# A gated linear-attention stage: where in program order the next head's set-up stands, and how many buffers its tiles have

## The chip, the cores and the metric

The kernel runs on one core of one Trainium2 chip. The core's engines work in parallel, each through its own list of instructions in a fixed order: PE (TensorE) multiplies matrices, DVE (VectorE) and ACT (ScalarE) work element by element, POOL (GpSimd) does further element-wise work, and SP only issues DMA transfers between the chip's memory (HBM) and the on-chip buffers. An instruction that has to wait holds back everything behind it on its engine. The metric is device time in microseconds (us) for one execution.

## The reference

Two blocks of two layers each run one after the other on 512 tokens of width 1024, in float32. The stage that is changed is in the second block. Each of its two layers is a SwiGLU feed-forward, then a mixer, then another SwiGLU. The mixer joins a neighbourhood attention (8 heads of width 64) and a gated linear attention (GLA, 4 heads, keys of width 64, values of width 128), and `w_out` projects both back to width 1024:

```
def step(state, inp):                      # one chunk of 64 tokens, per head
    qi, ki, vi, gi = inp
    b = cumsum(gi)                         # log decays
    inter = (qi * exp(b)) @ state
    decay = exp(where(mask, b[:, None] - b[None], -inf))
    a = einsum('td,sd,tsd->ts', qi, ki, decay)
    state = exp(b_last)[:, None] * state + (ki * exp(b_last - b)).T @ vi
    return state, inter + a @ vi
o = rmsnorm(gla(q, k, v, gf, forward) + gla(q, k, v, gb, backward)) * silu(r)
x = x + concat([neighbourhood_attention, o]) @ w_out
```

## The kernel before

Activations stay in on-chip memory as four tiles of 128 tokens. Every large product is done as three matmuls on a high and a low part of each operand (`mm3`, lines 150 to 152). The parts are made by a cast on ACT (`whi`, line 111) and a subtraction on DVE (`wlo`, line 112). Weights come by DMA into `raw` buffers (two of them, line 125) and are split from there.

The mixer stage is `mix`. It first projects the values (`gla_v`), the gates (`gates`, which leaves the summed log decays `b` of the four heads in tiles `gb`), `gla_q` and `gla_k` (one DRAM buffer, `gla_qk`) and the output gate (`gla_r`, with a Silu on ACT); v, q, k and r are written to DRAM and read back per head. Then `interleave` draws from two generators in turn, 36 steps of `heads()` against 24 of `others()`.

`heads()` runs `gla_head` for each of the four GLA heads. The forward direction is kept in partitions 0 to 63 and the backward direction in 64 to 127. One head has three parts, and 9 steps:

- **Set-up** (1 step, lines 1321 to 1363): four DMAs for q and k (`gq`, `gk`, each loaded twice, for the two directions) and one for v (`gv`); the shifted decays `gR` (two DVE copies and a POOL memset); `geq`, an exponential of `b` on ACT; the decays to the end of each 128-token block (`gd`, two DVE subtractions, lines 1337 and 1338), their exponential on ACT (line 1340) and its product with k on DVE (line 1341); four PE transposes, an ACT copy, four PE matmuls with v (line 1349); the states `gst` (six DVE instructions, lines 1353 to 1360, reading PSUM); and `gzi`, q times `geq` (line 1362).
- **Seven levels** (7 steps, lines 1366 to 1388): for block sizes 64, 32, ... 1 the scores between the two halves of each block. A level is a DVE subtraction (line 1370), two ACT exponentials into `ge` (1373, 1374), a POOL memset and two POOL products with k into `gzk` (1376 to 1378), a DVE product of `ge` with q in place (1379; it follows the POOL products, which read the same tile), PE matmuls (1383), and a masked DVE copy into `gA` (1387).
- **End** (1 step, lines 1389 to 1408): state and score matmuls (1391, 1392), the norm, the gate, transposes, and the split into a pair of `gkt` tiles for `w_out`.

`gq`, `gk`, `gR` and `geq` have one buffer each; `gd`, `gv`, `gzk`, `gzi` and `gst` have two, `ge` four. `others()` projects the neighbourhood attention's values (`tokens_out`, line 1161) and its q and k (`na_qk`, line 1181), loads what that attention needs (`na_setup`, 14 DMAs at line 1193), and then runs its first four heads (`na_heads`: scores 1238, transposes 1260, outputs 1267) beside the projection of GLA heads 0 and 1 through `w_out`.

The instructions are not issued in exactly the order in which the program writes them. A planner orders each engine's list when the kernel is built: an instruction written earlier has the higher priority, but the planner, going by its own estimates of durations, lets a later one go ahead when its operands and its tile's buffer are free first. A tile whose tag has one buffer can only be written when the last reader of the tile before it is through. On the chip the list is then fixed.

Of the kernel before, what the change touches and what calls it, by code (L numbers as in the profile page):

```python
# [10 lines left out]
F32 = mybir.dt.float32  # L11
# [6 lines left out]
S = 512  # L18
# [1051 lines left out]
GH = 4  # L1070
# [10 lines left out]
class Block2(Block1):  # L1081
# [5 lines left out]
    def gates(self, pool, l, w_in, hT):  # L1087

        nc = self.nc
        d = self.d  # L1090
        v = w_in[:, 3072:3104].rearrange("(k p) n -> p k n", p=P)
        raw = self.wpool.tile([P, 2048], F32, name=self.n("raw"), tag="raw", bufs=2)
        rv = raw[:, :1024].rearrange("p (k n) -> p k n", k=KD)
        with nc.allow_non_contiguous_dma(reason="32 columns"):
            for i in range(4):
                nc.sync.dma_start(rv[:, :, i * 32 : i * 32 + 32], v)
        w = self.wsplit([raw[:, :1024]])[0]
        gw = pool.tile([32, GH, 2, 64], F32, name=self.n("gw"), tag="gA")
        nc.gpsimd.memset(gw, 0.0)
        gb = pool.tile([P, GH], F32, name=self.n("gb"), tag="gbias")  # L1100
        with nc.allow_non_contiguous_dma(reason="gate weights"):
            for i, n in enumerate("fb"):
                nc.sync.dma_start(gw[i * 16 : i * 16 + 16, :, i, :], d[f"w_gate_{n}_2"][l].rearrange("r (h e) -> r h e", h=GH))
                nc.sync.dma_start(gb[i * 64 : i * 64 + 64, :], d[f"b_gate_{n}_2"][l].rearrange("(h e) -> e h", h=GH))
        scan = pool.tile([P, S], F32, name=self.n("scan"), tag="gst", bufs=2)
        nc.sync.dma_start(scan, d["c_scan"])
        ps = self.proj_T(w, hT)
        code = pool.tile([32, S], F32, name=self.n("code"), tag="gR")
        nc.scalar.copy(code, ps[:32])
        es, bs = [], []  # L1110
        for h in range(GH):
            z = self.ps(tag="BD")
            nc.tensor.matmul(z, gw[:, h].rearrange("r a e -> r (a e)"), code, start=True, stop=True)
            a = pool.tile([P, S], F32, name=self.n("gt"), tag="ge", bufs=4)
            nc.scalar.activation(a, z, AF.Abs, bias=gb[:, h : h + 1])
            m = pool.tile([P, S], F32, name=self.n("gb"), tag="gb", bufs=4)
            nc.vector.tensor_scalar(m, z, gb[:, h : h + 1], 0.0, ALU.add, ALU.min)
            es.append(a)
            bs.append(m)
        for a in es:  # L1120
            nc.scalar.activation(a, a, AF.Exp, scale=-1.0)
        for a in es:
            nc.scalar.activation(a, a, AF.Ln, bias=1.0)
        for a, m in zip(es, bs):
            nc.vector.tensor_sub(a, m, a)
            nc.vector.tensor_tensor_scan(m[:64], scan[:64], a[:64], 0.0, ALU.mult, ALU.add)
            nc.vector.tensor_tensor_scan(m[64:, ::-1], scan[64:, ::-1], a[64:, ::-1], 0.0, ALU.mult, ALU.add)
        return bs
# [189 lines left out]
    def gla_head(self, pool, h, b, qk, vs, rs, mask, sgn, kts, new_k):  # L1318
        nc = self.nc
        new = lambda tag, bufs: pool.tile([P, S], F32, name=self.n(tag), tag=tag, bufs=bufs)  # L1320
        q, k = new("gq", 1), new("gk", 1)
        for t, m in ((q, 0), (k, 256)):
            for i in range(2):
                nc.sync.dma_start(t[i * 64 : i * 64 + 64, :], qk[m + h * 64 : m + h * 64 + 64, :])
        v3 = pool.tile([P, NT, P], F32, name=self.n("gv"), tag="gv", bufs=2)
        nc.sync.dma_start(v3, vs[:, h * P : (h + 1) * P].rearrange("(t p) e -> p t e", p=P))
        R = new("gR", 1)
        nc.vector.tensor_copy(R[:64], b[:64])
        nc.vector.tensor_copy(R[64:, 0:511], b[64:, 1:512])
        nc.gpsimd.memset(R[64:, 511:512], 0.0)  # L1330

        eq = new("geq", 1)
        nc.scalar.activation(eq, b, AF.Exp, scale=1.0 / 16)
        D = new("gd", 2)
        bt = b.rearrange("p (t s) -> p t s", t=NT)
# [68 lines left out]
        k = new_k()  # L1404
# [4 lines left out]
    def mix(self, l, xs, norm, nxt):  # L1409
# [4 lines left out]
        with self.scope("mix") as pool:  # L1414
            new_k = lambda: Split(*(pool.tile([P, 512], F32R, name=self.n("gkt"), tag="gkt", bufs=10) for _ in range(2)))
            mask = pool.tile([P, len(LEVELS), P], I32, name=self.n("gmask"), tag="gmask")
            nc.sync.dma_start(mask, d["c_gmask"].rearrange("l p t -> p l t"))
            both = pool.tile([P, 8], F32, name=self.n("both"), tag="both")
            sgn, ngain = both[:, 0:2], both[:, 4:8]
            for i in range(2):  # L1420
                for c in range(2):
                    nc.gpsimd.memset(sgn[i * 64 : i * 64 + 64, c : c + 1], (1.0 if i == c else -1.0) / 16)
            gain = pool.tile([P, P], F32, name=self.n("ggain"), tag="ggain")
            nc.sync.dma_start(gain, d["gla_gain_2"][l].unsqueeze(0).to_broadcast([P, P]))
            with nc.allow_non_contiguous_dma(reason="512 gains"):
                nc.sync.dma_start(ngain, d["na_gain_2"][l].rearrange("(k p) -> p k", p=P))
            hT = norm.hT
            vs, rs, nv = (self.dr(n, [S, 512]) for n in ("gla_v", "gla_r", "na_v"))
            nqk = self.dr("na_qk", [8, P, S])
            for _ in self.tokens_out(pool, w_in, 2048, hT, vs, None, norm.finish):  # L1430
                pass
            bs = self.gates(pool, l, w_in, hT)
            qk = self.gla_qk(pool, w_in, hT)
            for _ in self.tokens_out(pool, w_in, 2560, hT, rs, gain):
                pass
            kts = []
            st = {}

            def gout(a, tag):
                ws = self.wrows(w_out, [512 + (a + i) * P for i in range(2)])  # L1440
                return self.down_steps(xs, [self.cols(k) for k in kts[a : a + 2]], ws, tag=tag)

            def heads():
                for h in range(GH):
                    yield from self.gla_head(pool, h, bs[h], qk, vs, rs, mask, sgn, kts, new_k)

            def others():
                yield from self.tokens_out(pool, w_in, 1024, hT, nv)
                yield from self.na_qk(pool, w_in, hT, nqk)
                st["na"] = self.na_setup(pool, l, nqk, nv)  # L1450
                g = gout(0, "A")
                for _ in range(4):
                    next(g)
                for _ in self.na_heads(pool, st["na"], (0, 1), new_k, "A", "C", "C"):
                    next(g, None)
                    yield
                for _ in g:
                    pass

            interleave(heads(), 36, others(), 24)  # L1460
            na = st["na"]
            interleave(self.na_heads(pool, na, (2, 3), new_k, "AB", "C", "D"), 8, gout(2, "AB"), 8)
            ws = self.wrows(w_out, [k * P for k in range(4)], scales=[ngain[:, k : k + 1] for k in range(4)])
            self.down(xs, [self.cols(k) for k in na["K"]], ws, self.na_scale(pool, na), nxt.after)
# [108 lines left out]
```

## Time and profile before

| | |
|---|---|
| time, median of 3 runs | 3266.24 us (3262.35 to 3266.77) |
| the profiled execution's own time | 3260.75 us |
| its span, first to last instruction | 3259.0 us |
| PE busy | 3194.2 us (98%) |
| DVE busy | 2168.5 us (67%) |
| ACT busy | 1391.3 us (43%) |
| POOL busy | 481.0 us (15%) |
| mean granted TensorE clock | 0.991 of full speed |

The two interleaved stretches lie at about 1660 to 1840 us and 2656 to 2840 us of the span. A busy PE is one with a matmul in flight; at a granted clock below 1.00 the same matmuls take longer and are still counted as busy, so idle time and clock have to be read side by side.

### The profile page before, as it was taken

The page shows a single profiled execution, that of the slowest core. Times are in us where ns is not written, and L with a number is a line of the kernel's source. Part 1 is how long each engine was busy: PE and PEld are TensorE (multiplying, and loading weights), DVE is VectorE, ACT ScalarE, POOL GpSimd, SP SyncE. Part 2 cuts the span into 40 slices and gives each one's busy share as a digit, 9 for nine tenths or more (in the row PEclk, how much of TensorE's full clock was granted, in tenths as well). Part 3 has the DMA queues.
Part 4 walks back from the last instruction along what each step waited for, and adds up shares of the span by engine and source line. Part 5 has one row for each costly group of instructions (what it writes and reads, how often), then busy time and mean ns, then how long its engine had stood idle before and what let it go on. Part 6 is the DMA issues. An engine that isn't in the chain of part 4 may idle for free. (4 is left out here: it accounts for less than half of the span.)

```text
span 3259.0 us, 39483 instructions
## 1 busy us (share of the span) xinstructions
PE 3194.2 (98%) x15381; PEld 2645.9 (81%) x15381; DVE 2168.5 (67%) x3054; ACT 1391.3 (43%) x2130; POOL 481.0 (15%) x554
## 2 busy tenths in 40 slices
PE   8999999999999999999999999999999999999999
PEld 8777888887788888888878788888888887788887
DVE  5566677767867776666576656665666657656665
ACT  5465444446744444333354533333333354443332
POOL 0022222111222210000134300000000025400000
PEclk9999999999999999999999999999999999999999
DMA  6311333222233323232444232324223253332231
GB/s 214 93 40 38 111 104 104 82 81 90 77 131 104 104 78 123 78 104 90 129 133 148 69 110 91 117 78 135 92 78 108 85 164 122 111 104 91 78 109 60
DMA packets 265882, 330.51 MB, mean 101 GB/s; under 512 B 20872, under 2 KB 198240, under 8 KB 265696
## 3 DMA queue, kind: packets, MB, share of 16 engines
q1 hardware_dynamic: 265696, 328.00, 31.2%
q8 instruction: 121, 1.98, 0.2%
q14 instruction: 65, 0.53, 0.1%
HBM read 313.28 MB, written 14.68 MB: 101 GB/s over the span
## 5 line engine op out<-in xcount | busy, mean ns | idle before, releaser
L111 ACT CAST whi<-raw 128x1024 fp32r<-128x1024 f32 x398 | 414.0, 1050 | 428.0 <-PE psC L152 128.7
L112 DVE TENSOR_TENSOR wlo<-raw,whi 128x1024 fp32r<-128x1024 f32 x402 | 499.1, 1247 | 116.4 <-ACT whi L111 108.6
L150 PE MATMUL psA<-hThi,wlo 128*128 128x512 f32 (+1 forms) x1264 | 473.2, 375 | 2.7 <-ACT hThi L111 1.8
L151 PE MATMUL psA<-hTlo,whi 128*128 128x512 f32 (+1 forms) x1264 | 472.1, 374 | 0.8 <-DVE hTlo L112 0.7
L150 PE MATMUL psC<-hThi,wlo 128*128 128x512 f32 (+1 forms) x1264 | 471.2, 373 | 0.5 <-ACT hThi L111 0.5
L152 PE MATMUL psA<-hThi,whi 128*128 128x512 f32 (+1 forms) x1264 | 471.2, 373 | 0.0
L151 PE MATMUL psC<-hTlo,whi 128*128 128x512 f32 (+1 forms) x1264 | 470.5, 372 | 0.0
L152 PE MATMUL psC<-hThi,whi 128*128 128x512 f32 (+1 forms) x1264 | 470.1, 372 | 0.0
L111 ACT CAST whi<-b 128x1024 fp32r<-128x1024 f32 (+1 forms) x238 | 237.6, 998 | 283.7 <-PE psA L152 91.7
L112 DVE TENSOR_TENSOR wlo<-b,whi 128x1024 fp32r<-128x1024 f32 (+1 forms) x238 | 275.8, 1159 | 68.5 <-ACT whi L111 66.8
L172 POOL TENSOR_TENSOR rv<-msv,mhalf 128x1 f32<-128x1 f32 (+1 forms) x60 | 45.7, 762 | 1737.8 <-DVE msv L169 1737.8
L150 PEld LDWEIGHTS psA<-hThi,wlo 128*128 128x128 f32 x1264 | 239.3, 189 | 45.8 <-ACT hThi L111 4.8
L151 PEld LDWEIGHTS psA<-hTlo,whi 128*128 128x128 f32 x1264 | 239.2, 189 | 43.9 <-DVE hTlo L112 2.5
L152 PEld LDWEIGHTS psA<-hThi,whi 128*128 128x128 f32 x1264 | 239.1, 189 | 41.3
L151 PEld LDWEIGHTS psC<-hTlo,whi 128*128 128x128 f32 x1264 | 238.4, 189 | 42.0 <-issue 0.8
L150 PEld LDWEIGHTS psC<-hThi,wlo 128*128 128x128 f32 x1264 | 238.4, 189 | 41.9 <-ACT hThi L111 1.0
L152 PEld LDWEIGHTS psC<-hThi,whi 128*128 128x128 f32 x1264 | 238.3, 189 | 41.3
L359 DVE SCALAR_TENSOR_TENSOR x<-psB,x 128x512 f32<-128x512 f32 x272 | 181.0, 686 | 136.2 <-PE psB L152 135.2
L150 PE MATMUL psB<-whi,kb 128*128 128x512 f32 x608 | 238.0, 391 | 0.0
L151 PE MATMUL psB<-wlo,kb 128*128 128x512 f32 x608 | 236.7, 389 | 0.0
L152 PE MATMUL psB<-whi,kb 128*128 128x512 f32 x608 | 236.6, 389 | 0.0
L359 DVE SCALAR_TENSOR_TENSOR x<-psD,x 128x512 f32<-128x512 f32 x204 | 135.9, 686 | 112.4 <-PE psD L152 112.4
(506 smaller groups left out, 5783.8 us busy)
## 6 DMA issues: line engine op xcount, KB each, us to landing
raw<-in_ffn_wg_dram SPq DMA_DIRECT2D x44, 1024.0 KB
raw<-in_ffn_wu_dram SPq DMA_DIRECT2D x44, 1024.0 KB
b<-in_ffn_wd_dram SPq DMA_DIRECT2D x72, 512.0 KB
raw<-in_w_up_dram SPq DMA_DIRECT2D x32, 1024.0 KB
b<-in_w_down_dram SPq DMA_DIRECT2D x56, 512.0 KB
raw<-in_w_in_dram SPq DMA_DIRECT2D x40, 512.0 KB
raw<-in_w_out_dram SPq DMA_DIRECT2D x32, 512.0 KB
raw<-in_lru_w_in_dram SPq DMA_DIRECT2D x10, 1024.0 KB
```

The costliest lines, as they stand in the source:

```text
L111: self.nc.scalar.copy(out.hi, src)
L112: self.nc.vector.tensor_sub(out.lo, src, out.hi.bitcast(F32))
L150: nc.tensor.matmul(out, lhsT.lo, rhs.hi, start=start, stop=False, skip_group_check=more)
L151: nc.tensor.matmul(out, lhsT.hi, rhs.lo, start=False, stop=False, skip_group_check=more)
L152: nc.tensor.matmul(out, lhsT.hi, rhs.hi, start=False, stop=stop, skip_group_check=more)
L172: nc.gpsimd.tensor_tensor(r, ms, e, ALU.pow)
L359: nc.vector.scalar_tensor_tensor(x, p, scale, x, ALU.mult, ALU.add)
```

## The change

The generators of all four heads are made at once. Head 0's set-up comes first; then each head's steps are drawn as before, but after the level with index 2 the set-up of the next head is drawn. The number of steps stays 36. `gq`, `gk`, `gR` and `geq` get two buffers (8 KB more per partition in all); `code` in `gates` shares the tag `gR` and is given the same count.

```diff
@@ gates
-        code = pool.tile([32, S], F32, name=self.n("code"), tag="gR")
+        code = pool.tile([32, S], F32, name=self.n("code"), tag="gR", bufs=2)
@@ gla_head
-        q, k = new("gq", 1), new("gk", 1)
+        q, k = new("gq", 2), new("gk", 2)
...
-        R = new("gR", 1)
+        R = new("gR", 2)
...
-        eq = new("geq", 1)
+        eq = new("geq", 2)
@@ mix, heads()
+                gens = [self.gla_head(pool, h, bs[h], qk, vs, rs, mask, sgn, kts, new_k) for h in range(GH)]
+                next(gens[0])
+                yield
                 for h in range(GH):
-                    yield from self.gla_head(pool, h, bs[h], qk, vs, rs, mask, sgn, kts, new_k)
+                    for i, _ in enumerate(gens[h]):
+                        yield
+                        if i == 2 and h + 1 < GH:
+                            next(gens[h + 1])
+                            yield
```

## Rows read from the trace of the kernel before

**Rows 1.** The page's busy times by engine: us, share of the span, instructions.

```profile
PE 3194.2 (98%) x15381; PEld 2645.9 (81%) x15381; DVE 2168.5 (67%) x3054; ACT 1391.3 (43%) x2130; POOL 481.0 (15%) x554
```

**Rows 2.** Engine timeline of PE: start, us, instruction, [idle before it and its releaser].

```profile
1701.84 2.05 PE L1383 MATMUL psB<-ge,gzk 128*128 128x128 f32 x8 [3.52 <-DVE ge L1379]
...
1703.54 0.77 PE L150 MATMUL psC<-whi,hTlo 128*128 128x512 f32 x1
...
2700.60 2.00 PE L1383 MATMUL psB<-ge,gzk 128*128 128x128 f32 x8 [3.51 <-DVE ge L1379]
```

**Rows 3.** 4-us stretches: length; PE, PEld, DVE, ACT, POOL busy (count); PEclk; DMA share; GB/s.

```profile
1700.00:1704.00 4.00, 2.17 (x9) 2.20 (x10) 4.00 (x5) 0.83 (x3) 1.14 (x1) 0.57 0.25 66
...
1704.00:1708.00 4.00, 4.00 (x12) 3.11 (x12) 4.00 (x6) 0.88 (x2) 2.32 (x3) 0.58 0.49 135
...
2700.00:2704.00 4.00, 3.40 (x12) 3.14 (x13) 4.00 (x6) 0.91 (x2) 1.19 (x2) 0.58 0.22 66
```

**Rows 4.** Timeline of DVE, first of the two layers.

```profile
1680.59 1.23 DVE L112 TENSOR_TENSOR wlo<-raw,whi 128x1024 fp32r<-128x1024 f32 x1 [6.50 <-ACT whi L111]
...
1695.43 0.68 DVE L1337 TENSOR_TENSOR gd<-gb 64x512 f32<-64x512 f32 x1
...
1696.12 1.25 DVE L1338 TENSOR_TENSOR gd<-gb 64x512 f32<-64x512 f32 x1
...
1697.40 1.22 DVE L1370 TENSOR_TENSOR gd<-gb,gR 128x512 f32<-128x512 f32 x1
...
1699.16 1.28 DVE L1370 TENSOR_TENSOR gd<-gb,gR 128x512 f32<-128x512 f32 x1
...
1700.37 1.32 DVE L1379 TENSOR_TENSOR ge<-ge,gq 128x512 f32<-128x512 f32 x1
...
1707.56 0.68 DVE L1341 TENSOR_TENSOR ge<-ge,gk 128x512 f32<-128x512 f32 x1
...
1723.64 0.35 DVE L1360 SCALAR_TENSOR_TENSOR gst<-gst,geq,psD 64x128 f32<-64x128 f32 x1
```

**Rows 5.** Timeline of ACT around the same gap.

```profile
1697.48 0.63 ACT L1340 ACTIVATE ge<-gd 128x512 f32<-128x512 f32 x1 [5.73 <-PE psA L152]
...
1698.02 1.98 ACT L111 CAST whi<-raw 128x1024 fp32r<-128x1024 f32 x2
```

**Rows 6.** Timeline of POOL around the same gap.

```profile
1696.87 1.20 POOL L1378 TENSOR_TENSOR gzk<-gk,ge 64x256 f32<-64x256 f32 x1
```

**Rows 7.** Timeline of PE where the neighbourhood attention begins, both layers.

```profile
1794.16 1.13 PE L1238 MATMUL psA<-hTlo,hThi 64*128 64x256 f32 x4 [2.13 <-DMA hThi<-na_qk]
...
2794.46 2.07 PE L1238 MATMUL psA<-hTlo,hThi 64*128 64x256 f32 x4 [4.20 <-DMA hThi<-na_qk]
```

**Rows 8.** 4-us stretches behind these two waits.

```profile
1796.00:1800.00 4.00, 4.00 (x11) 2.38 (x10) 3.80 (x10) 1.09 (x4) 3.69 (x4) 0.52 0.73 259
...
1800.00:1804.00 4.00, 4.00 (x18) 3.24 (x17) 2.20 (x6) 1.57 (x5) 2.37 (x3) 0.63 0.02 4
...
2792.00:2796.00 4.00, 1.54 (x4) 1.17 (x4) 0.00 (x0) 0.00 (x0) 0.00 (x0) 0.60 0.83 220
...
2796.00:2800.00 4.00, 4.00 (x11) 2.45 (x10) 2.75 (x7) 1.09 (x4) 3.16 (x4) 0.54 0.69 238
```

**Rows 9.** Timeline of SP (DMA issues): one early stretch, and before that wait.

```profile
1668.24 6.87 SPq L125 DMA_DIRECT2D raw<-in_w_in_dram  x4
...
1781.60 6.22 SPq L1193 DMA_DIRECT2D hThi<-na_v  x10
...
1787.87 0.45 SPq L1225 DMA_DIRECT2D hThi<-na_qk  x1
...
1788.41 1.12 SPq L1324 DMA_DIRECT2D gq<-gla_qk  x2
```

**Rows 10.** Timeline of PE: two levels of the last head in the neighbourhood attention.

```profile
1814.97 1.95 PE L1383 MATMUL psB<-ge,gzk 128*128 128x128 f32 x16
```

**Rows 11.** A 4-us stretch in the neighbourhood attention of the second layer.

```profile
2844.00:2848.00 4.00, 4.00 (x17) 3.58 (x18) 1.88 (x10) 1.28 (x3) 0.00 (x0) 0.50 0.00 0
```

## The prediction

> **What bounds the kernel now.** I read the page's busy times first, then the waits of PE, then stretches of 4 us with the granted clock, and last the timelines of the other engines around each PE gap. PE is busy for 98% of the span [rows 1], and the sum of the matmuls does not change here. So only two things can be won or lost: time in which PE stands idle, and time in which it runs at the lower of its two clock levels (1.2 instead of 2.4 GHz), which follows a gap. In the two mixer stages these sit at few places, and two of them touch what is moved.
>
> Place A is inside the levels of head 0, in both layers. PE idles 3.52 and 3.51 us before a level's score matmuls, released by the DVE product of line 1379 [rows 2]. The granted clock falls at once: 0.57 and 0.58 over two stretches of 4 us in the first layer, 0.58 over one in the second [rows 3]. A stretch at clock c loses (1 - c) x 4 us of full-speed work: 1.72 + 1.68 + 1.68 = 5.1 us. With the idle time A holds 3.52 + 3.51 + 5.1 = 12.1 us.
>
> Place B is where the neighbourhood attention begins: PE waits 2.13 and 4.20 us for its q tile from DRAM [rows 7], and then runs at 0.52 and 0.63 in the first layer, 0.60 and 0.54 in the second [rows 8]: 1.92 + 1.48 + 1.60 + 1.84 = 6.8 us of lost clock. The 0.60 row holds part of the wait itself, so that is a little high; B holds about 2.13 + 4.20 + 6.8 = 13.1 us.
>
> **What makes place A.** The planner already draws head 1's set-up forward, but only when head 0 has released its single `gR` and `ge` and `gd` buffers. The two subtractions of lines 1337 and 1338 then run at 1695.43 and 1696.12, in the middle of head 0's last levels, and head 1's first level subtractions follow at 1697.40 and 1699.16 [rows 4]. The product of line 1379 for head 0's next level has its POOL operand at 1696.87 + 1.20 = 1698.07 [rows 6], yet starts at 1700.37, since it is queued behind these. ACT is held too: its list has the exponential of line 1340 next, which starts at 1697.48, right after line 1338 ends at 1697.37, after 5.73 us of idling; the row names an old PE release, but what came last is the subtraction. Two weight casts are queued behind it [rows 5], and PE's next weights come from these, at 1703.54 [rows 2]. So one late set-up holds both of the things that PE could do next.
>
> **The change, part by part.**
>
> *Set-up earlier, in two buffers (place A).* Head 1's set-up is now written after head 0's third level, and with a second `gR` it need not wait for head 0's last level subtraction. What leaves the crowded stretch: two subtractions, 0.68 + 1.25 = 1.93 us as they ran there, and two copies into `gR`, of the same 64 partitions x 512 and so about 0.68 each by the row of line 1337, 1.4 together: 3.3 us of DVE. What may enter, because the products and states of head 1 now come before head 0's levels 3 to 6 as well: two products of 0.68 and six state instructions of at most 0.35 each [rows 4], 1.4 + 2.1 = 3.5 us. On DVE's sum that is a draw. The gain depends on some of it going into the 6.50 us in which DVE idled at 1674 to 1680 [rows 4], and on ACT's exponential being ready when its turn comes. The best case: line 1379 starts at 1698.07, ends 0.68 later at 1698.75 (the row of line 1341, the same shape); PE ran dry at 1701.84 - 3.52 = 1698.32. So 0.4 us of gap stays per layer, and if so short a gap leaves the clock alone, 12.1 - 0.8 = 11.3 us are won. The worst case within this step is 0: another set-up instruction stands in the same place. I take 8, nearer to the upper end, because the hold of ACT's list goes away with the early subtraction, whatever DVE's sum does.
>
> *The same for the last head (place B).* q and k of head 3 are issued at 1788.41, behind ten of `na_setup`'s DMAs and the attention's q [rows 9], because the single `gq` was still read by head 2. With two buffers and the new place in the program, head 3's loads come before `na_setup`: by the draw of 36 steps against 24 the set-up of head 3 is step 23, and `others()` reaches `na_setup` and the first attention unit at its step 17, when 25 steps of `heads()` have been drawn. (Before, the set-up was step 28.) The DMA wait itself does not shrink, since the attention's q was issued ahead of `gq` already. What changes is that PE has something to do in it: a level is 0.98 us of matmuls by the row of two levels in 1.95 [rows 10], and two to five ready levels fill 2.13 and 4.20 us. Fully filled, B gives up to 13.1; not filled at all, 0. Whether the planner places the levels ahead of the waiting matmul depends on its own estimate of that DMA, so I take half, 6.5.
>
> *What it costs.* Work that fills B is taken from the attention units behind it, where head 3's levels stand between the units now. I put 2 us against that; the bound is in the rival below. The set-up's DMAs are four issues of about 0.56 (1.12 for two [rows 9]) and one for v: 2.2 to 2.8 us on SP, now in front of some weight loads. SP spends 6.87 us on four weight issues at 1668.24 [rows 9], far more than four issues take, so it waits there for `raw` buffers and a further issue in that wait costs nothing; if that cover is gone, the next weights come up to 2.8 us later, once per layer, 5.6 in all. I take 0. The second `geq`, `gR` for `code` and 8 KB more per partition cost no instruction; where tiles of the following stage now lie over those of the mixer, a wait could arise that no row shows. I take 0 for it, with the 0.3 to 0.4 us of a short PE gap as one end and one gap of A's size, 3.5 us plus clock, as the other.
>
> **A rule weighed against the rows.** Line 1337 took 0.68 us and line 1338, of the same shape, 1.25. Line 1370 took 1.22 at 1697.40 while POOL's product of line 1378 ran from 1696.87 to 1698.07 [rows 4, 6]: the DVE instruction ended 0.55 us after POOL's did, as if it had stood still until then. The Trainium skill, page "SBUF — State Buffer", section "Who interferes with whom", says that DVE with two on-chip inputs and a reading GpSimd instruction share a port pair, that whoever starts first keeps it for its whole instruction, and that the other fully blocks. The trace agrees by that row. By that rule moving DVE work among POOL's products can cost more than its own duration, which speaks against this change; as a mechanism of this kernel it is a rival below.
>
> The sum: -8 - 6.5 + 2 = -12.5 us. Against the profiled execution's own 3260.75 us that is 3248.3. That execution is 5.5 us under the median of the runs, so against the median the forecast is 3266.24 - 12.5 = 3253.7, say 3254.
>
> **Rivals.**
>
> *All of it.* A and B are both emptied, nothing is given back: -11.3 - 13.1 = -24, and with 2 to 4 us of small new gaps about -20: 3246. For it: all rows of A and B name resources that are doubled or loaded earlier. Against it: the planner fixes each list by its own estimates, and new lists have new gaps.
>
> *It does not do what it says.* The planner had already drawn the set-up forward, and the DVE draw of 3.3 against 3.5 leaves A as it was; B's matmul keeps its place in PE's list. About -2: 3264.
>
> *The lock eats it.* Six instructions per set-up with two on-chip inputs or a copy (two copies, two subtractions, two products) each lose 1.25 - 0.68 = 0.57 us beside POOL's products: 3.4 us for a head, where DVE is late once per layer, 6.8 in all. Of -12.5 about -5 is left: 3261. For it: the rows above. Against it: four of the six already run beside POOL.
>
> *Slower: the attention loses its filler.* After B the attention units form a chain (scores, softmax, transposes, outputs), and PE is kept busy in it by head 3's seven levels, 7 x 0.98 = 6.9 us, and the projection. If the levels have all run by the time the projection's first part is through, the later units wait for their own chain: at most 6.9 us of idling per layer, and a gap there can drop the clock, as one did in the second layer (0.50 over a stretch of 4 us [rows 11], 2 us lost in that row alone, and two or three such rows). With 6.9 + 4 = 11 per layer and only A won, -8 + 22 = +14; with half of that idling and of the clock +3. I take +8: 3274. It decides from the point where more than half of the levels run before the second attention unit. For it: the low-clock stretch shows that this part has little to spare. Against it: the levels are written at the same steps as before, and only their operands are there earlier.
>
> **Chances.** Forecast 0.42, all of it 0.12, does nothing 0.16, the lock 0.10, slower 0.20. About 0.2%, 6.5 us, is what a measurement of this kernel can tell from no change. Faster by more than that holds the forecast without a little of its edge, and all of it: 0.52. No difference holds the two middle rivals and that edge: 0.27. Slower: 0.21, the rival and a wait that I have not seen. The forecast's own range is 3248 to 3260 (A between 5 and 11, B between 3 and 11, give-back up to 4). The range over the cases is 3243 to 3274, which leaves out the far part of "all of it" and the worse half of the slower one.
>
> **What would show it.** Step A is right if PE has no gap over 1 us before line 1383 in head 0's levels and the clock stays at 1.00 there; if line 1338 for head 1 runs before 1690 us or so; and if ACT's casts of line 111 are not behind line 1340. Step B is right if head 3's `gq` loads are issued before the DMAs of line 1193, and levels of head 3 stand on PE before the first attention scores. The slower rival shows as PE waits of line 1260, 1267 or 1238 on ACT or DVE after 1800 us with clock below 1.00. The forecast is wrong if the gaps of A and B are still there, or if as much idle time has come up elsewhere in the two mixer stages; it would also be wrong if anything outside them moves.

## The result, and the profile after

The change made the kernel slower. The changed kernel takes 3284.44 us (median, 3277.56 to 3294.62) against 3264.30 us (3257.58 to 3267.95) of the kernel before on the same chip: ratio 1.0065, 95% interval [1.0043, 1.0087]. Run again on another chip the changed kernel took 3280.60 us, 1.0048 [1.0031, 1.0066]. The forecast was 3254 us, with a range of 3243 to 3274, so the sign was wrong as well.

The profiled execution of the changed kernel has its own time of 3279.57 us and a span of 3277.8 us, 18.8 us more than the span before. Its busy times, which answer to [rows 1]:

```profile
PE 3205.9 (98%) x15381; PEld 2652.2 (81%) x15381; DVE 2164.6 (66%) x3054; ACT 1393.9 (43%) x2130; POOL 486.7 (15%) x554
```

PE has the same 15381 instructions and is busy for 11.7 us longer, which is the clock. The next views are of the two mixer stages (first gate projection to the attention's last output), in one stretch each; columns as in [rows 3]. First the kernel before, then the changed kernel.

```profile
1634.30:1873.00 238.70, 228.66 (x1212) 185.95 (x1212) 166.55 (x322) 119.18 (x281) 94.07 (x118) 0.97 0.36 114
2631.40:2877.10 245.70, 233.31 (x1212) 189.56 (x1212) 165.50 (x322) 119.15 (x281) 93.40 (x118) 0.95 0.35 110
```

```profile
1637.40:1885.20 247.80, 232.67 (x1208) 187.87 (x1208) 163.86 (x322) 119.59 (x281) 95.39 (x117) 0.95 0.35 109
2644.40:2895.10 250.70, 235.37 (x1208) 189.67 (x1208) 163.49 (x321) 119.74 (x281) 95.49 (x117) 0.95 0.34 108
```

The stages take 484.4 us before and 498.5 after, 14.1 more. PE's idle time is the length less the busy time: 22.4 before, 30.5 after. The rest is the clock, which the following views place. Of the 18.8 us, 3.1 came before the first mixer, in code that the change does not touch, and 1.6 between the stages and behind them.

**Where PE waits now.** PE's timeline of the first layer, with idle time and releaser; the second layer repeats it (0.48, 4.03, 2.12, 2.17, 1.18 and 3.53 us).

```profile
1694.71 1.13 PE L1383 MATMUL psB<-ge,gzk 128*128 128x128 f32 x8 [0.48 <-DVE ge L1379]
...
1717.27 0.79 PE L1392 MATMUL psD<-gv,gA 128*128 128x128 f32 x2 [4.03 <-DVE gA L1387]
...
1763.94 0.33 PE L1403 MATMUL psD<-ident,ev 128*128 128x128 f32 x1 [2.12 <-DVE ev L1402]
...
1799.51 0.49 PE L1392 MATMUL psD<-gv,gA 128*128 128x128 f32 x2 [2.17 <-DVE gA L1387]
...
1814.15 0.33 PE L1403 MATMUL psD<-ident,ev 128*128 128x128 f32 x1 [1.34 <-DVE ev L1402]
...
1849.51 0.48 PE L1403 MATMUL psD<-ident,ev 128*128 128x128 f32 x1 [3.82 <-DVE ev L1402]
```

The gaps of [rows 2] are down to the 0.48 us of the first row, and the DMA waits of [rows 7] are gone. In their place stand, in the order of the other rows, the output of head 0 behind its last masked copy, the end of head 1, the output of head 2, the end of head 2 and the end of the last head. An end (lines 1402 and 1403) is the product with 1/rms and r on DVE and the transposes that follow.

**Where the clock falls.** Stretches of 4 us of the changed kernel, behind head 0's output, where the attention begins, and behind the last head's end:

```profile
1716.00:1720.00 4.00, 2.73 (x13) 2.73 (x14) 2.99 (x5) 0.00 (x0) 0.00 (x0) 0.50 0.55 157
1720.00:1724.00 4.00, 4.00 (x15) 3.02 (x15) 1.65 (x6) 1.44 (x9) 1.43 (x3) 0.69 0.59 178
...
1800.00:1804.00 4.00, 4.00 (x24) 3.09 (x23) 2.28 (x8) 0.18 (x1) 1.44 (x2) 1.00 0.84 296
...
1848.00:1852.00 4.00, 2.49 (x5) 1.36 (x6) 2.57 (x10) 0.00 (x0) 0.00 (x0) 0.60 0.01 3
1852.00:1856.00 4.00, 4.00 (x18) 3.16 (x18) 0.41 (x2) 0.73 (x2) 0.00 (x0) 0.50 0.00 2
1856.00:1860.00 4.00, 4.00 (x16) 3.06 (x15) 2.11 (x8) 2.62 (x9) 2.06 (x3) 0.50 0.02 4
1860.00:1864.00 4.00, 4.00 (x20) 3.41 (x19) 1.19 (x5) 0.59 (x1) 0.00 (x0) 0.69 0.32 131
```

Behind the last head's end 1.60 + 2.00 + 2.00 + 1.24 = 6.8 us of full-speed work are lost, and as much in the second layer (granted clock 0.89, 0.50, 0.50, 0.50, 0.90 from 2856 to 2876 us). Where the attention begins, the clock is 1.00 now, against [rows 8].

The account of both layers together, in us, idle time and lost clock taken from such rows:

| place | idle | clock | sum |
|---|---|---|---|
| A, inside head 0: the old gaps gone | -7.0 | -5.1 | -12.1 |
| head 0's output, 4.03 each | +8.1 | +5.1 | +13.2 |
| B, attention's DMA wait gone | -6.3 | -6.8 | -13.1 |
| head 2's output, 2.17 each (0.60 before) | +3.1 | 0 | +3.1 |
| ends of heads 0 to 2, gaps under 0.6 | +4.6 | +1.7 | +6.3 |
| last head's end (0.85 and 0.86 before) | +5.6 | +8.6 | +14.2 |
| gates at the stages' start, unchanged code | 0 | +3.4 | +3.4 |

They come to +15.0 against the 14.1 by which the stages grew; the stretches after hold eight matmuls fewer (x1208 against x1212, twice), some 0.2 us each, which is of that size. The last head's end alone is as large as the whole difference.

**What holds the last head's end.** SP's timeline (issues) before, then after:

```profile
1836.33 0.39 SPq L1395 DMA_DIRECT2D ev<-gla_r  x1
1839.04 0.39 SPq L247 DMA_DIRECT2D raw<-in_ffn_wu_dram  x1
```

```profile
1839.50 0.63 SPq L1208 DMA_DIRECT2D rpb<-in_na_rpb_dram  x1
1840.26 0.39 SPq L247 DMA_DIRECT2D raw<-in_ffn_wu_dram  x1
1840.75 0.52 SPq L1395 DMA_DIRECT2D ev<-gla_r  x1
```

And DVE's timeline of the changed kernel:

```profile
1849.10 0.61 DVE L1402 SCALAR_TENSOR_TENSOR ev<-psD,rv,ev 128x128 f32<-128x128 f32 x2 [4.87 <-DMA ev<-gla_r]
```

The last head's r, 256 KB, is now issued behind a 1 MB weight load of the feed-forward that follows the mixer. It releases DVE 8.35 us after its issue (1849.10 - 1840.75). DVE stands at the product meanwhile. PE stands at the transposes that read the product (line 1403), with the attention's next scores (line 1238, at 1849.92) behind them in its list. The Trainium skill, page "DMA: Bandwidth & Descriptors", section "Queues, rings and completion order", says that each DMA engine consumes one queue's descriptors in order. The trace agrees so far that r's reader was released only at 1849.10, and that 1.45 MB were moved from 1840 to 1849 us, about the size of r, the weights and a third load together. That third load, the attention's bias table (line 1208, 132.5 KB), was issued 0.76 us ahead of the weights; how much of the 8.35 us is the weights' and how much the table's is not shown.

**What holds head 0's output.** DVE's timeline of the changed kernel, between the last product and the last masked copy of head 0:

```profile
1709.11 0.69 DVE L1379 TENSOR_TENSOR ge<-ge,gq 128x512 f32<-128x512 f32 x1 [1.06 <-POOL gzk L1378]
1709.72 0.69 DVE L1370 TENSOR_TENSOR gd<-gb,gR 128x512 f32<-128x512 f32 x1
1710.32 1.22 DVE L1337 TENSOR_TENSOR gd<-gb 64x512 f32<-64x512 f32 x1
1711.55 1.13 DVE L1338 TENSOR_TENSOR gd<-gb 64x512 f32<-64x512 f32 x1
1712.72 0.74 DVE L1387 COPY_PREDICATED gA<-gmask,psB 128x512 f32<-128x512 int32 x1
1713.35 0.97 DVE L1370 TENSOR_TENSOR gd<-gb,gR 128x512 f32<-128x512 f32 x1
1714.24 1.20 DVE L1379 TENSOR_TENSOR ge<-ge,gq 128x512 f32<-128x512 f32 x1
1715.37 1.21 DVE L112 TENSOR_TENSOR wlo<-raw,whi 128x1024 fp32r<-128x1024 f32 x1
1716.50 0.71 DVE L1387 COPY_PREDICATED gA<-gmask,psB 128x512 f32<-128x512 int32 x1
```

The masked copy at 1716.50 is the one that PE waits for. The subtractions at 1710.32 and 1711.55 are head 2's set-up, the products and subtractions around the copy at 1712.72 are head 1's first levels. The planner draws two heads ahead, and these instructions stand in front of head 0's last copies as head 1's set-up did before.

POOL's timeline for the same time:

```profile
1709.74 1.25 POOL L1377 TENSOR_TENSOR gzk<-gk,ge 64x256 f32<-64x256 f32 x1
1711.07 1.07 POOL L1378 TENSOR_TENSOR gzk<-gk,ge 64x256 f32<-64x256 f32 x1
...
1713.05 0.72 POOL L1377 TENSOR_TENSOR gzk<-gk,ge 64x256 f32<-64x256 f32 x1
1713.82 1.07 POOL L1378 TENSOR_TENSOR gzk<-gk,ge 64x256 f32<-64x256 f32 x1
```

DVE's instructions at 1710.32, 1711.55, 1713.35 and 1714.24 each end 0.54 or 0.55 us after one of these four products. They took 1.22, 1.13, 0.97 and 1.20 us, where the same lines take 0.68 or 0.69 at 1667.76, 1668.45, 1709.72 and 1709.11: some 1.8 us more together.

### The profile page after: what moved, and what is told of

It reads as the page before. It is cut to its first block, busy times and chain, and to the rows that moved or that the text cites. A ratio compares the mean times of both kernels' runs of the same rounds, so it can differ in the third digit from the quotient of the medians.

```text
span 3277.8 us, 39509 instructions
## 1 busy us (share of the span) xinstructions
PE 3205.9 (98%) x15381; PEld 2652.2 (81%) x15381; DVE 2164.6 (66%) x3054; ACT 1393.9 (43%) x2130; POOL 486.7 (15%) x554
## 4 chain that ended last, share of the span: by engine, by line
PE 90%; DVE 3%; issue 2%; ACT 2%; POOL 2%; DMA 1%; SPq 0%; POOLq 0%; DVEq 0%; ACTq 0%
PE psA L150 9%; PE psA L151 9%; PE psA L152 9%; PE psC L150 9%; PE psC L152 9%; PE psC L151 9%; PE psB L150 5%; PE psB L151 5%; PE psB L152 5%; PE psD L150 5%; PE psD L151 5%; PE psD L152 4%; PE psB L1383 1%; PE psA L1238 1%; DMA ev<-gla_r 1%
## 5 line engine op out<-in xcount | busy, mean ns | idle before, releaser
L150 PE MATMUL psC<-hThi,wlo 128*128 128x512 f32 (+1 forms) x1264 | 472.0, 374 | 0.5 <-ACT hThi L111 0.5
L150 PE MATMUL psB<-whi,kb 128*128 128x512 f32 x608 | 238.0, 391 | 0.0
```

The source lines that it names most:

```text
L150: nc.tensor.matmul(out, lhsT.lo, rhs.hi, start=start, stop=False, skip_group_check=more)
```

## Experiments

The ratios are to the kernel before, run beside each on the same chip, with 95% intervals; they need not be the quotient of two medians. Two theories ran through them. D: the set-up amid the levels crowds DVE in front of a head's last copies. R: the late load of r at the last head's end is the price.

**One half at a time.** Only the buffers (the old loop over the heads put back):

```diff
             def heads():
-                gens = [self.gla_head(pool, h, bs[h], qk, vs, rs, mask, sgn, kts, new_k) for h in range(GH)]
...
+                for h in range(GH):
+                    yield from self.gla_head(pool, h, bs[h], qk, vs, rs, mask, sgn, kts, new_k)
```

> The buffer counts of the change with the old order of heads(). Theory R (the last head's load of its gate r stands in SP's list behind a 1 MB weight load of the next feed-forward, and PE waits for it): the list has that swap here too, so a PE gap of 3 to 4 us before line 1403 of the last head with 10 us of low clock behind it, in both layers, about +14 us; against it the attention's DMA wait of the kernel before (place B) is gone, about -10. Together 0 to +6 us against the kernel before. Theory D (the set-up written amid the levels crowds DVE in front of the last levels): here the set-up is not written there, so no gap before line 1392 of head 0, no gap at the last head, and about -10 us.

Measured 3263.28 us, 0.9988 [0.9973, 1.0004]. A's gaps are there in full (3.51 us each), so the buffers do not touch them; B's wait is gone. SP's list has the last head's r behind the FFN weights already, but the last head's end waits only 1.42 and 2.14 us; R had put 3 to 4 there, D none. Head 2's subtractions (line 1337 at 1735.21) stand behind head 0's last copy. Buffers alone are neither gain nor loss.

Only the place (`q, k = new("gq", 1), new("gk", 1)`, `R = new("gR", 1)`, `eq = new("geq", 1)`, `code` without `bufs=2`):

> The new order of heads() with the old, single buffers. SP's list has the swap of r and the weights. Theory R: slower than the kernel before by 5 to 20 us, with the late r load at the last head. Place B: q of head 3 is single-buffered again, but its set-up is written earlier; the attention's DMA wait may come back (2 to 4 us). If only the two buffers together with the order cost time, it is within 5 us of the kernel before.

Measured 3273.95 us, 1.0014 [0.9997, 1.0030]. A's gap is 1.05 us, but the transposes of the set-up (line 1344) wait 1.41, 2.44 and 0.51 us in the first layer and 2.24, 2.73 and 3.47 in the second, for DVE's product of line 1341. r is behind the weights here too, and the last head's end waits 0.99 us in the first layer and under 0.4 in the second. Head 2's subtractions (lines 1337 and 1338 at 1712.34 and 1713.02) stand in front of head 0's last copy (1714.80), with single buffers: it is the place, not the second buffers, that draws them there. Neither half is as slow as both together.

**r's load.** Ahead of the fourth level instead of at the head's end, with buffers of its own, in the changed kernel and in the kernel before. In kernels with this edit line numbers behind it are up to 3 higher (1395 is 1392, 1404 is 1403).

```diff
         for li, c in enumerate(LEVELS):
+            if li == 3:
+                r3 = pool.tile([P, NT, P], F32, name=self.n("gr3"), tag="gr3", bufs=2)
+                nc.sync.dma_start(r3, rs[:, h * P : (h + 1) * P].rearrange("(t p) e -> p t e", p=P))
...
-        r3 = pool.tile([P, NT, P], F32, name=self.n("ev"), tag="ev", bufs=4)
-        nc.sync.dma_start(r3, rs[:, h * P : (h + 1) * P].rearrange("(t p) e -> p t e", p=P))
```

> The changed kernel with the load of r written before level 3 of its head, into two buffers of its own instead of the shared ev ring. Theory R: the gap before line 1403 of the last head falls from 3.8 and 3.5 us to under 1 us, the low-clock stretch behind it goes, and the time falls by 10 to 14 us against the changed kernel, to 3270 to 3275, with the 4.0 us gap before line 1392 of head 0 unchanged. Theory D: the last head's gap stays over 3 us since DVE is what is late; 3280 or more.

> The kernel before with the same early load of r. Theory R: r was not late there (its load stood ahead of the weights, gap 0.85 us), so within 4 us of the kernel before. If the early load by itself is worth something, it would be faster by more than 6 us, and the gain of the run with the changed kernel would not belong to the swap.

In the changed kernel: 3265.82 us, 0.9995 [0.9978, 1.0012], below the time that R expected; in the kernel before: 3262.64 us, 0.9990 [0.9973, 1.0007]. So the edit gives the kernel before nothing that can be measured, and brings the changed one level with it. The gap at the last head's end is 1.19 us in both layers, the one at the end of head 2 is gone, and the stretches of the first layer that answer to the ones above stay at full clock:

```profile
1844.00:1848.00 4.00, 2.81 (x17) 1.80 (x15) 2.39 (x9) 2.53 (x9) 2.96 (x4) 1.00 0.71 240
1848.00:1852.00 4.00, 4.00 (x25) 2.99 (x24) 2.44 (x12) 2.31 (x7) 0.00 (x0) 1.00 0.02 7
```

Head 0's output still waits 4.03 us. So the change without its late load comes out even, not ahead.

r where the change has it, only in buffers of its own:

```diff
-        r3 = pool.tile([P, NT, P], F32, name=self.n("ev"), tag="ev", bufs=4)
+        r3 = pool.tile([P, NT, P], F32, name=self.n("gr3"), tag="gr3", bufs=2)
```

> The changed kernel with one edit: r's tile has two buffers of its own, its load stays at the same place in the program. Theory R, in its sharper form (r's tile comes from the shared ev ring of four, and waiting for a free one is what lets the weight load pass it): SP's list now has r's load ahead of the feed-forward's weights, so the last head's gap before line 1403 falls under 1.5 us and the time to 3263 to 3270, as with the early load. If the later step of the end in the program is what matters, not the ring: within 5 us of the changed kernel's 3284.

Measured 3272.31 us, 1.0022 [1.0005, 1.0038]. SP's list has r ahead of the weights again, and the last end's gap is 1.20 us, the other gaps as in the kernel with the early load. Sharing the ring `ev` of four tiles is thus what pushed r back. The time is between that kernel's and the changed one's and just outside the expected range, although the gaps are the same. What differs is the clock: its median over the executions is 0.9885 here and 0.9905 with the early load. By this run a third or more of the loss is still there when r is on time, though its interval overlaps with that of the early load.

Last, the late load in the kernel before. There the last head's load is written behind its mean squares, which on SP is that one exchange:

```diff
-        nc.sync.dma_start(r3, rs[:, h * P : (h + 1) * P].rearrange("(t p) e -> p t e", p=P))
+        if h < GH - 1:
+            nc.sync.dma_start(r3, rs[:, h * P : (h + 1) * P].rearrange("(t p) e -> p t e", p=P))
...
         r = self.rstd(ss, P, NT)
+        if h == GH - 1:
+            nc.sync.dma_start(r3, rs[:, h * P : (h + 1) * P].rearrange("(t p) e -> p t e", p=P))
```

> The kernel before, with one edit: the last head's r load is written after its mean squares, so that in SP's list it stands behind the first FFN weight load instead of ahead of it, as in the changed kernel. Nothing else of the change is in. The planner answers by writing the eight transposes of line 1260 and the last score matmuls ahead of the head's end on PE. R (the place of r's load by itself is the price): DVE's products at the head's end are released by r's DMA some 8 us after its issue, PE idles 2 to 4 us before the transposes of the head's end in both layers, low clock behind it; 8 to 18 us more than before, ratio 1.0025 to 1.0055. Rival (the late load costs only where PE's list has nothing else in front of the end): DVE is released by the DMA just as late, but PE's gap stays under 1.5 us; within 3 us of before, ratio 0.999 to 1.001. D (only the crowd on DVE in the levels matters): no change, same ratio as the rival's, and no wait of DVE for r.

Measured 3256.74 us, 0.9987 [0.9971, 1.0004]: R as put there fell. The time fits the rival and D alike. What separates them is a wait of DVE for r at the last head's end, and there is none in either layer, so the rival's own condition, r just as late, did not come. Timelines of SP and then of DVE in this kernel (here 1402, 1405 and 1406 are the lines of r's load, the product and the transposes):

```profile
1843.78 0.39 SPq L247 DMA_DIRECT2D raw<-in_ffn_wu_dram  x1
1844.27 0.52 SPq L1402 DMA_DIRECT2D ev<-gla_r  x1
```

```profile
1849.99 0.42 DVE L1241 CUSTOM_DVE_ANT_0 hTlo<-psA,h 128x256 f32<-128x256 f32 x1 [0.20 <-PE psC L1260]
...
1850.35 0.86 DVE L1405 SCALAR_TENSOR_TENSOR ev<-psD,rv,ev 128x128 f32<-128x128 f32 x3
```

r is issued the same 0.49 us behind the weights as in the changed kernel, but it was there within 6.08 us (1850.35 - 1844.27); the bias table was issued 3.50 us ahead of the weights here. DVE and PE have the attention's softmax and scores ahead of the head's end in their lists, and PE does not wait there at all. Since the planner answered the edit with these other lists, the run is no test of the exchange alone. Five kernels have r behind the weights, and their gaps before line 1403 of the last head, first and second layer, are 3.82 and 3.53 us (the changed kernel), 2.38 and 2.11 (set-up after level 5, below), 1.42 and 2.14 (buffers only), 0.99 and under 0.4 (place only), and none (this one). So what the late load costs depends on when it lands and on what the lists have in front of the instructions that need it.

**Where the set-up stands.** With r early, after the level with index 3, 4 or 5; then after 2 for head 1's set-up and after 4 for the others; and index 5 without the early r. The edit is the one line (`i == 5`, and so on):

```diff
-                        if i == 2 and h + 1 < GH:
+                        if i == 4 and h + 1 < GH:
```

> The changed kernel with the set-up of the next head drawn after the level with index 5 instead of 2, and the early load of r. By DVE's list the subtractions for head 2 now stand behind the end of head 0. Theory D: the gap of 4.0 us before line 1392 of head 0 falls under 1 us with its low clock, 7 us less per layer than the run with the changed order and early r: about 3258 to 3262, a little under the kernel before. Theory R alone: the same as that run, 3270 to 3275.

> The changed kernel with the set-up after the level with index 5, r left as it is (SP's list still has the weights ahead of it). Theory R prices the swap by itself: against the same kernel with the early r load (3256.6) it is slower by 10 to 18 us, with a gap of 3 us or more before line 1403 of the last head. If the place of the set-up was the cause of the slow-down and r only a companion: within 5 us of 3256.6.

> The early r load and the set-up after the level with index 4. By DVE's list head 1's subtractions stand ahead of head 0's first masked copy (place A gone) and head 2's behind head 0's last masked copy (no gap before the end's score matmuls of head 0). Theory D: no gap over 1 us in head 0, 5 to 8 us less than with the set-up after level 5 (3256.6): 3249 to 3253. If DVE's total in that stretch decides, not the order: the gap only moves to another level, within 3 us of 3256.6.

> The early r load and every set-up after level 3: head 2's subtractions stand ahead of head 0's last masked copy, as in the changed kernel. Theory D: the gap stays over 3 us, the time stays with the changed kernel with early r (3262 to 3267). If the later place alone helps, by steps: halfway, 3257 to 3261.

> The early r load; head 1's set-up after head 0's level 2 as in the changed kernel, those of heads 2 and 3 after level 4 of the head in front. In DVE's list head 1's part is as in the changed kernel, but head 2's two subtractions now stand behind head 0's last masked copy. Theory D (these two subtractions, 1.22 + 1.13 us in the trace of the changed kernel, are what holds that copy): PE's gap before the end's score matmuls of head 0 falls from 4.0 to between 1.5 and 2.5 us, and the time to that of the run with all set-ups after level 4, 3254 (3251 to 3258). If head 1's own early set-up is what crowds DVE there: the gap stays at 4 us and the time at 3262 or more.

| set-up after level | r | us | ratio, 95% interval | head 0's output waits, us |
|---|---|---|---|---|
| 2 (the change, run again) | as changed | 3280.60 | 1.0048 [1.0031, 1.0066] | 4.03 |
| 5 | as changed | 3268.10 | 1.0014 [0.9997, 1.0031] | 2.36 (a level's scores) |
| 2 | early | 3265.82 | 0.9995 [0.9978, 1.0012] | 4.03 |
| 3 | early | 3274.73 | 1.0031 [1.0013, 1.0050] | 3.87 |
| 4 | early | 3253.94 | 0.9963 [0.9948, 0.9978] | 2.39 |
| 5 | early | 3256.57 | 0.9979 [0.9962, 0.9996] | 2.35 (a level's scores) |
| 2, then 4 | early | 3260.55 | 0.9984 [0.9968, 1.0000] | 3.01 |

Theory D priced these runs only in part. After level 5 the gap before line 1392 is gone, but a level's scores wait 2.35 us instead. After level 4 it expected no gap over 1 us and 3249 to 3253; 2.39 us are left, and the time is just above. With 2 and then 4 both sides missed: the gap is 3.01 us, neither 1.5 to 2.5 nor 4, and the time 3260.55 is between theirs. After level 5 with r late the time is 11.5 us above that with r early, as R priced it, though on another chip; the last head's end waits 2.38 and 2.11 us and not 3.

> The changed kernel once more, beside these on one chip, to price r's late load under the same conditions: 3278 to 3288, that is 12 to 20 us over the same kernel with the early r load; 3.5 to 3.8 us of gap before line 1403 of the last head, followed by low clock, in both layers. If it comes out under 3274, most of the difference measured before between chips was not the kernel's.

Level 4 with r early beats both kernels: 3253.94 us (3249.87 to 3261.89). Its DVE timeline at head 0's last copy:

```profile
1712.51 1.21 DVE L1382 TENSOR_TENSOR ge<-ge,gq 128x512 f32<-128x512 f32 x1
1713.75 0.73 DVE L1390 COPY_PREDICATED gA<-gmask,psB 128x512 f32<-128x512 int32 x1
1714.37 0.67 DVE L1337 TENSOR_TENSOR gd<-gb 64x512 f32<-64x512 f32 x1
```

Head 2's first subtraction comes behind the copy here, and takes 0.67 us instead of 1.22. In the kernel with 2 and then 4 it is behind the copy too, with 3.01 us; with 3 it is ahead of it, with 3.87. So by the gaps with 2 and with 2 and then 4, which differ in this place alone, the two subtractions are worth 1.0 of the 4.03 us; with head 1's set-up later as well it is 1.6. The rest, by the rows above, is head 1's levels and a weight split. The stages of the kernel with level 4:

```profile
1638.10:1872.40 234.30, 224.67 (x1208) 181.78 (x1208) 163.90 (x321) 119.01 (x281) 95.61 (x117) 0.99 0.36 116
2631.80:2869.50 237.70, 227.78 (x1208) 184.59 (x1208) 163.45 (x322) 118.93 (x281) 95.90 (x117) 0.98 0.36 114
```

472.0 us against 484.4 before. Its idle time, 9.6 + 9.9 = 19.5, is only 2.9 less than before; the rest is nearly all granted clock, 0.99 and 0.98. Level 3 is the miss in this row of runs: its median is 9 us above that of level 2 with the early r, while in the profiles its idle time is 23.4 against 24.3 us and its stages are even shorter (238.0 + 245.5 against 241.6 + 244.7). The profile is of the fastest of its twelve executions, 3263.14 us at a granted clock of 0.992; the slowest took 3288.41 us at 0.983, some 2.8 us for each 0.001. The median clock is 0.9875 against 0.9905 with level 2, so by that rate 8 of the 9 us are clock. Why the clock was lower, and whether the chip has a part in it (the two ran on different ones), is open.

## Why the prediction was wrong

**What bounds the kernel** held. The matmuls took the same work, and idle time and clock in the two mixer stages make up 14.1 of the 18.8 us. The sign that the prediction named for being wrong came: as much idle time elsewhere in these stages (30.5 us against 22.4).

**What makes place A** held in its rows, but not in its cause. It put the late subtractions down to single buffers, and named `ge` and `gd` among them, which have four and two. With second buffers alone A's gaps are there in full (3.51 us), with the new place alone they are 1.05 us.

**Place A** failed, by its own worst case. The forecast took 8 of 12.1 us. The signs it named did come: the old gap is 0.48 us in both layers, and head 1's subtractions ran at 1667.76 and 1668.45, long before 1690 as expected. But the sentence that gave the worst case, "another set-up instruction stands in the same place", is what the trace shows: head 2's, in front of head 0's last copy, and the subtractions and products of head 1's levels with it. 12.1 us went, 13.2 came. I had counted 3.3 against 3.5 us of DVE as a draw and yet taken a gain, since I looked at head 1's set-up alone and did not follow the planner to the head after it. The draw was none, either: the two copies into `gR` took 0.42 and 0.73 us and stood at 1690.07 and 1690.51, ahead of the crowded stretch.

**Place B** came out by another mechanism. Head 3's loads were issued at 1748.80 to 1750.66, before the DMAs of line 1193 at 1784.96, as expected. But no levels of head 3 fill the wait: in front of the first scores (1801.49) PE has two matmuls of line 1383 for head 3 (0.39 us at 1801.18), not the two to five levels of the prediction. The attention's q was issued at 1794.80, and the scores start 6.69 us later without waiting (6.29 us later in the kernel before, with the wait). In that time PE does the last two levels of head 2 (from 1795.17) and, after a gap of 2.17 us, head 2's output. SP's and PE's timelines of the changed kernel:

```profile
1794.80 0.45 SPq L1225 DMA_DIRECT2D hThi<-na_qk  x1
```

```profile
1801.18 0.39 PE L1383 MATMUL psB<-ge,gzk 128*128 128x128 f32 x2
1801.49 1.13 PE L1238 MATMUL psA<-hTlo,hThi 64*128 64x256 f32 x4
```

The gap of 2.17 us is made on DVE, where level subtractions for head 3 (line 1370 at 1796.92 and 1798.13) stand in front of head 2's last copies. So the wait went partly into another gap at the same place. That the clock stayed at 1.00 behind it, 6.8 of B's 13.1 us, nothing in the prediction explains. What was given back is 3.1 us at head 2's output and 6.3 at the ends of heads and small gaps, 9.4 for 2 forecast. B less what it gives back is -3.7 us against -6.5 + 2 = -4.5, near only by luck.

The end of head 1, for instance, has its 1/rms step on DVE (line 169) queued behind two level instructions of head 2 (lines 1379 and 1370) and two of head 3's set-up (lines 1341 and 1362):

```profile
1759.76 0.69 DVE L1379 TENSOR_TENSOR ge<-ge,gq 128x512 f32<-128x512 f32 x1 [0.62 <-POOL gzk L1378]
1760.37 0.69 DVE L1341 TENSOR_TENSOR ge<-ge,gk 128x512 f32<-128x512 f32 x1
1760.97 0.68 DVE L1362 TENSOR_TENSOR gzi<-gq,geq 128x512 f32<-128x512 f32 x1
1761.58 0.69 DVE L1370 TENSOR_TENSOR gd<-gb,gR 128x512 f32<-128x512 f32 x1
1762.18 0.16 DVE L169 TENSOR_SCALAR msv<-ssv 128x4 f32<-128x4 f32 x1
```

**What it costs** is the step that set the sign. It said of the second buffers that "a wait could arise that no row shows", and took 0 for it; the wait that arose is r's, and the last head's end cost 14.2 us more in the profiled execution. I followed the DMAs of the set-up through SP's queue, and not the load that stays at the head's end. Its tile comes from the ring `ev`, which other tiles of the stage share; in the new lists its turn came after the first FFN weight load was issued, and buffers of its own put it ahead again. The runs show the price as the difference of pairs with and without the late load: 3280.60 or 3284.44 against 3265.82 (15 to 19 us, on different chips), and for level 5 3268.10 against 3256.57 (12 us). With r in its own buffers, 3272.31, it is 8 to 12 us. The late load on the kernel before, which cost nothing, shows that this price is not the queue's alone. Without the 14.2 us the terms of A and B leave 1.1 - 3.7 = -2.6 us, about what the run with r early shows (0.9995), and not -12.5: so the lost gain is place A's.

**The rivals.** The slower one had the right side and the wrong place: the units after 1800 us did not lack work, they stood behind one product on DVE and its transposes on PE. "It does not do what it says" was wrong for A, whose old gap went, and nearer for B, where the first scores stand almost where they stood in PE's list. The lock is seen and is a part: four instructions in front of head 0's last copy ended 0.54 or 0.55 us after a product of POOL, as line 1370 did in [rows 4, 6], and lost some 1.8 us in all, an estimate from the rows above. That level 4 with r early takes 3253.94 us, the forecast's own number, is luck: it is another kernel.

**Settled and open.** Shown: without its late r the changed kernel measures 0.9995 or 1.0022 and not 1.0048 to 1.0065, so the late r is most of the loss; and a late r can cost nothing where the lists are others. Shown by rows, and for the two subtractions by a run: what stands in front of head 0's last copy. Not settled: what the late r would cost in the kernel before with its lists unchanged; why r took 8.35 us in one kernel and at most 6.08 in another; why the same gaps cost more clock in one execution than in another, and so the 9 us between the kernels with levels 2 and 3, and the 6 between r early and r in its own buffers.

## What to carry to other kernels

When a step is moved ahead, follow every load that stays behind too: a small load that slips behind a large one on the same queue can come too late for its reader (here 8.35 us after its issue), and it is the reader that stands in an in-order list with other work behind it that turns this into idle time. A planner that is given the next iteration earlier draws from the one after it as well, with or without second buffers, so check the next-but-one iteration's instructions in front of the one that the busy engine waits for. Try the place of a step at several positions together with early loads: here index 4 gave 0.9963 and index 3 gave 1.0031.

## What the runs showed of the hardware that was not expected

Gaps of the same length cost very different amounts of clock. In the kernel before, PE idles 0.85 us at the last head's end of the first layer and 0.86 in the second. Behind the second the clock is at its lower level ([rows 11]; 5.1 us lost by 2856), behind the first it stays at the upper one:

```profile
1844.00:1848.00 4.00, 4.00 (x25) 3.02 (x25) 2.99 (x15) 2.04 (x5) 0.09 (x1) 1.00 0.02 6
1848.00:1852.00 4.00, 4.00 (x30) 3.51 (x28) 2.66 (x10) 2.12 (x8) 1.98 (x3) 1.00 0.20 71
```

In the kernel before, the clock was at 0.52 and 0.63 behind the wait of 2.13 us for the attention's q [rows 8]; in the changed kernel it stayed at 1.00 behind the 2.17 us in front of head 2's output, 2 us ahead of the same scores. The kernels with r early and with r in its own buffers have the same main gaps within 0.02 us in the first layer, and first stages of 241.6 and 247.8 us. Two profiled executions of the changed kernel have second stages of 250.7 and 247.7 us. Before the first mixer, in code that is the same in all kernels, 8.5 to 24.0 us of clock were lost in the profiled executions. So one profile can't tell kernels apart that differ by some 6 us in a stage or some 15 in the whole; the medians of many runs can tell smaller differences.
